# A hybrid decoder layer: expert down weights loaded by row blocks, and another order of the last gate chunk

## The chip, the cores and the metric

The kernel runs on one core of one Trainium2 chip. Its metric is the device time of one execution in microseconds (us). Five engines work on their own queues, each in the order of its instructions: TensorE (PE, with its weight loads as PEld), VectorE (DVE), ScalarE (ACT), GpSimd (POOL) and SyncE (SP), which issues nearly all loads. Data goes by 16 DMA engines between the chip's main memory and the on-chip memory.

## The reference

One decoder layer in float32 for 256 tokens of 2048 channels. What matters for the change is its second half:

```python
h = h + mixed @ w_out                       # conv and attention groups
xt = rms_norm(h, norm_ffn)
# each token: best of 4 groups, then the best 2 of the 8 experts in it
y_e = (silu(xt @ w_gate[e]) * (xt @ w_up[e])) @ w_down[e]      # e of 32, 2048 -> 512 -> 2048
h = h + sum over a token's two experts of weight * y_e
gate = sigmoid(rms_norm(h, norm_ple) @ w_ple_gate)             # 2048 x 2048
out = h + gate * (p @ w_ple)
```

All weights are read once: 479 MB in all, of which the experts have 403 MB.

## The kernel before

**Waves.** The 32 experts go in eight waves of four (`NW`). Each expert gets up to 32 tokens, gathered by a matmul with a selection matrix. The four experts of a wave share TensorE's array, each with its own group of 32 columns, so a product over four experts is four short matmuls side by side. A wave first makes gate and up (`gate_up`, L971), then the down product: hidden values of 512 channels, in four row blocks `j` of 128, against `w_down[e]`. For waves 0 to 3 the whole down product follows at once. For waves 4 to 7 only its first 1024 output columns do (`down_rows`, L1031); the other two chunks of 512 columns are made after wave 7 (`down_wave`, L1115), wave by wave, first chunk 2 (columns 1024 to 1535), then chunk 3. Each wave's result goes through `outputs` (a high part `yh` by ScalarE, a low part `yl` by VectorE, L1071 and L1072) and `scatter` (L1078), which returns it to token order in PSUM. `add_down` (L1123) adds a chunk's sum to the residual `acc`.

**The gate product.** It is made in chunks of 512 input rows: as soon as a chunk of the residual is final, `rows` transposes it (L1151) and splits it into a high and a low part `hs` (L1154, L1157, L1158); `squares` adds up its squares. A chunk has eight gate steps, numbered 0 to 23 over chunks 0 to 2 here and 24 to 31 in the last chunk: four column blocks `n` of 512, times two halves `q`. A step (`gate_step`, L1176 to L1178) is 12 matmuls of 512 columns, on a piece of `w_ple_gate` that `split` has divided into a high part (ScalarE copy, L347) and a low part (VectorE subtraction, L348). I call these split 0 to 31, by their steps. `prep_pg` issues the splits up to a given one, into three slots `wsl` used in turn; a split waits until the step that used its slot is done. After a column block of chunks 0 to 2 its sums are added to `gs` (L1202).

**Order at the end.** `steps(n)` issues the next `n` gate steps between other work. The gate steps of chunks 0 to 2 lie between the down products of waves 4 to 7. In the last chunk, `preload` (L1281) puts the `gs` collected so far into PSUM by a float32 matmul with the identity, two tiles per column block; the gate steps add to it. Then, per column block and token half: sigmoid (ScalarE, L1306), multiply by the `p` product (L1307), add to the residual (L1308), and a DMA to the output. The sigmoid's scale `rs5` needs the squares of all chunks: a reduction (L1291), a square root, a reciprocal, with a table load before the sigmoid.

**Slots and loads.** The on-chip memory has a ring of 26 slots of 1 MiB (`NSLOT`). `want` lists the loads in order, each 1 MiB; `free` gives slots back in program order and at once issues the next loads of the list on SP (L76). So a load is issued behind the release that its place in the program gives it. The list for waves 4 to 7: for each wave, gate and up, then eight half loads of `w_down` (first 1024 columns; one expert, two row blocks each, pieces of 4 KB); after wave 7, four column loads per wave and chunk (one expert, four row blocks each, pieces of 2 KB), with pairs of `w_ple_gate` loads between them by the list `halves_`.

**Nothing is reordered by a planner**: the kernel is written under a manual schedule, and each engine's instructions in the trace stand in the order in which the code issues them.

Of the kernel before, what the change touches and what calls it, by code (L numbers as in the profile page):

```python
# [8 lines left out]
F32R = mybir.dt.float32r  # L9
# [14 lines left out]
NSLOT = 26  # L24
# [6 lines left out]
def kernel(ctx: ExitStack, tc: tile.TileContext, I, out):  # L31
# [104 lines left out]
                         wt[e].rearrange("(p j) f -> p j f", j=16)[:, 4 * j4:4 * j4 + 4, :])  # L136

    def want_d(w, c0, n):
        for e in range(4 * w, 4 * w + 4):
            want(("d", e, c0), [128, 4, n], w_down[e].rearrange("(j p) n -> p j n", p=128)[:, :, c0:c0 + n])  # L140

    def want_rows(w):
        for j in range(4):
# [1 line left out]
                want(("r", e, j), [128, D], w_down[e, 128 * j:128 * j + 128, :])  # L145

    def want_halves(w):
        for jp in range(2):
            for e in range(4 * w, 4 * w + 4):
                want(("r", e, jp), [128, 2, 1024],  # L150
                     w_down[e, 256 * jp:256 * jp + 256, 0:1024].rearrange("(j p) n -> p j n", p=128))

    TC = [(0, 512), (512, 512), (1024, 512), (1536, 512)]
    w_pg_v = w_pg.rearrange("(k p) n -> p k n", p=128)
# [17 lines left out]
                want(("ple", k), [128, 2048], w_ple[128 * k:128 * k + 128, :])  # L172

    order = [(2, w) for w in range(NROW, NW)] + [(3, w) for w in range(NROW, NW)]
    halves_ = [(0, 1), (1, 0), (1, 1), (2, 0), None, (2, 1), None, (3, 0)]
    for (ci, w), nxt_ in zip(order, halves_):
        want_d(w, *TC[ci])
        if nxt_:
# [840 lines left out]
    def down_rows(w):  # L1019

        hv = hTw(w).rearrange("p (j s) -> p j s", j=4)
        nn = 4 if w < NROW else 2
        pts = [ps() for _ in range(nn)]

        def block(j, n):
            for e in range(4):
                if w < NROW:
                    d = arrived["r", 4 * w + e, j]
                else:
                    d = arrived["r", 4 * w + e, j // 2][:, j % 2]  # L1030
                nc.tensor.matmul(pts[n][32 * e:32 * e + 32, :], hv[:, j, 32 * e:32 * e + 32],  # L1031
                                 d[:, 512 * n:512 * n + 512], start=j == 0, stop=j == 3, tile_position=(0, 32 * e))

        def sums(n, y):
            ns = slice(512 * n, 512 * n + 512)
            po = pa()
            scatter(po, w, y, True, True)
            for tt in range(2):
                if w == 0:
                    if n == 0:  # L1040
                        macc[tt] = alloc([128, D], F32, "macc")
                    nc.vector.tensor_copy(macc[tt][:, ns], po[:, tt])
                else:
                    to = (hmid if w == NW - 1 else macc)[tt][:, ns]
                    nc.vector.tensor_add(to, po[:, tt], to)

        if w == NW - 1:
            for j in range(4):
                block(j, 0)
            y = outputs(pts[0], w)  # L1050
            for j in range(4):
                if j == 2:
                    sums(0, y)
                block(j, 1)
            free(8)
            y = outputs(pts[1], w)
            rows(0)
            sums(1, y)
            return
        for j in range(4):  # L1060
            for n in range(nn):
                block(j, n)
            if w < NROW or j % 2:
                free(4)
        for n in range(nn):
            sums(n, outputs(pts[n], w))

# [41 lines left out]
    def down_wave(w, c0, cn):  # L1109

        pt = ps()
        hv = hTw(w).rearrange("p (j s) -> p j s", j=4)
        for j in range(4):
            for e in range(4):
                nc.tensor.matmul(pt[32 * e:32 * e + 32, :], hv[:, j, 32 * e:32 * e + 32],  # L1115
                                 arrived["d", 4 * w + e, c0][:, j, :],
                                 start=j == 0, stop=j == 3, tile_position=(0, 32 * e))
        free(4)
        return outputs(pt, w)

    def add_down(po, c0, cn):
# [137 lines left out]
    rows(2)  # L1259
    steps(1)  # L1260
    squares(2)
    steps(3)
    po = pa()
    for w in range(NROW, NW):
        y = down_wave(w, *TC[3])
# [5 lines left out]
        scatter(po, w, y, w == NROW, w == NW - 1)  # L1271
        if w < NW - 1:
            steps(1)
    assert not todo
    early = [two(0), None, two(1), None]

    def preload(n):
        if early[n] is None:
            early[n] = two(n // 2)
        for tt in range(2):  # L1280
            nc.tensor.matmul(early[n][tt], ident, gs[tt][:, 512 * n:512 * n + 512], start=True, stop=False)  # L1281

    ci = last
    preload(0)
    add_down(po, *TC[ci])
    rows(ci)
    prep_pg(ci, 1)
    preload(1)
    preload(2)
    squares(ci)  # L1290
    nc.vector.tensor_reduce(rs5, ss5[:, :, 0:4], axis=AX.X, op=OP.add)  # L1291
    nc.scalar.activation(rs5, rs5, AF.Sqrt, bias=eps, scale=1.0 / D)
    nc.scalar.activation(junk, eps, AF.Sigmoid)
    nc.vector.reciprocal(rs5, rs5)
    so = [alloc([128, 4, 512], F32, "so") for _ in range(2)]
    for n in range(4):
        if n == 3:
            preload(3)
        for q in range(2):
            prep_pg(ci, 2 * n + q + 1)  # L1300
            gate_step(ci, 2 * n + q, early[n], False)
            prep_pg(ci, 2 * n + q + 2)
        ns = slice(512 * n, 512 * n + 512)
        for tt in range(2):
            sg = so[tt][:, n]
            nc.scalar.activation(sg, early[n][tt], AF.Sigmoid, scale=rs5[:, tt])  # L1306
            nc.vector.tensor_mul(sg, sg, ple[tt][:, ns])  # L1307
            nc.vector.tensor_add(sg, sg, acc[tt][:, ns])  # L1308
            nc.sync.dma_start(out[128 * tt:128 * tt + 128, ns], sg)
# [132 lines left out]
```

## Time and profile before

| | us |
|---|---|
| three runs | 1362.24, 1362.25, 1362.37 (median 1362.25) |
| the profiled execution | 1362.01 |
| its span, first to last instruction | 1360.3 |
| TensorE busy | 1137.8 (84%) |
| VectorE busy | 410.6 (30%) |
| ScalarE busy | 265.8 (20%) |
| DMA: 484.29 MB, mean 356 GB/s | |

Busy times overlap: they say how much an engine did, not what the end waited for. In the page's forty slices the DMA engines are full from about 380 us to 1320 us, and TensorE is nearly full again in the last 150 us. So the end of the kernel has to be read in the timeline of its last stage, engine by engine.

### The profile page before, as it was taken

The numbers are of one execution on the slowest core, as the hardware profiler recorded it, in microseconds if no ns is written. First come the engines' busy times: TensorE is split into PE (matmuls) and PEld (weight loads), VectorE is DVE, ScalarE is ACT, GpSimd is POOL, SyncE is SP. The second block draws the span as 40 slices with busy tenths as digits, with TensorE's granted clock in tenths as the row PEclk, the third lists the DMA queues.
The fourth block names the chain that finished last, engine by engine and source line by source line (L and its number), as shares of the span: only waits on it lengthen the run. The fifth ranks groups of instructions, "written<-read, shape, count | busy, mean of one in ns | idle before, by whom it ended". The sixth has DMA issues, their size and how long they took to land.

```text
span 1360.3 us, 14996 instructions
## 1 busy us (share of the span) xinstructions
PE 1137.8 (84%) x6171; PEld 633.3 (47%) x6172; DVE 410.6 (30%) x623; ACT 265.8 (20%) x435; POOL 122.6 (9%) x150
## 2 busy tenths in 40 slices
PE   8999899999998787668677775966986876689997
PEld 7888778888663251215125121511531511136655
DVE  6747877655411210201111020110110120124536
ACT  6435455544101000000000000000010000024324
POOL 2214577100000000000000000000000000000000
PEclk9999999999998888889879879998988988889999
DMA  8992245976899999999999999999999999999981
GB/s 261 311 343 80 77 154 175 376 240 221 345 421 420 421 421 421 421 422 420 422 421 421 422 421 422 414 420 421 414 420 421 415 420 422 414 396 394 392 339 63
DMA packets 133141, 484.29 MB, mean 356 GB/s; under 512 B 12020, under 2 KB 49292, under 8 KB 92876
## 3 DMA queue, kind: packets, MB, share of 16 engines
q1 hardware_dynamic: 131916, 480.37, 89.6%
q0 software_dynamic: 864, 2.40, 0.5%
q8 instruction: 50, 0.82, 0.2%
q10 hardware_dynamic: 288, 0.52, 0.2%
q14 instruction: 23, 0.19, 0.0%
HBM read 478.80 MB, written 4.19 MB: 355 GB/s over the span
## 4 chain that ended last, share of the span: by engine, by line
DMA 48%; PE 40%; DVE 5%; ACT 3%; issue 2%; SPq 1%; POOL 1%; ACTq 0%; DVEq 0%; POOLq 0%
DMA ld<-in_w_up_dram 33%; DMA ld<-in_w_down_dram 14%; PE pat L774 7%; PE pst L955 5%; PE pat L971 4%; PE pat L775 3%; PE pat L752 2%; PE pat L754 2%; PE pat L753 2%; PE pst L1115 2%; SPq L76 1%; PE pst L1098 1%; PE pst L1031 1%; DVE wsp L348 1%; PE pat L1078 1%
## 5 line engine op out<-in xcount | busy, mean ns | idle before, releaser
L971 PE MATMUL pat<-ld,xg 128*32 128x512 f32 x2048 | 328.2, 674 | 105.7 <-DMA ld<-in_w_up_dram 60.7
L971 PEld LDWEIGHTS pat<-ld,xg 128*32 128x32 f32 x2048 | 77.1, 121 | 345.9 <-issue 154.6
L774 PE MATMUL pat<-xs,wsp 128*128 128x512 f32 x544 | 197.1, 404 | 0.0
L1031 PE MATMUL pst<-ld,wv 128*32 128x512 f32 x768 | 151.9, 777 | 47.5 <-DMA ld<-in_w_down_dram 42.7
L775 PE MATMUL pat<-xs,wsp 128*128 128x256 f32 x544 | 154.0, 283 | 1.5 <-DVE wsp L348 1.5
L348 DVE TENSOR_TENSOR wsp<-ld,wsp 128x1024 fp32r<-128x1024 f32 x91 | 131.0, 1444 | 74.8 <-ACT wsp L347 74.8
L957 DVE TENSOR_TENSOR xg<-pst,gffn 128x512 f32<-128x512 f32 (+1 forms) x33 | 22.3, 676 | 400.1 <-PE pst L955 400.1
L347 ACT CAST wsp<-ld 128x1024 fp32r<-128x1024 f32 x104 | 107.9, 1048 | 87.2 <-PE pat L754 43.9
L955 PEld LDWEIGHTS pst<-sel,x 128*128 128x128 f32 x512 | 112.7, 311 | 8.4 <-issue 5.0
L774 PEld LDWEIGHTS pat<-xs,wsp 128*128 128x128 f32 x544 | 103.5, 190 | 27.8 <-issue 2.9
L955 PE MATMUL pst<-sel,x 128*128 128x128 f32 x512 | 114.8, 384 | 0.0
L1031 PEld LDWEIGHTS pst<-ld,wv 128*32 128x32 f32 x768 | 33.0, 135 | 160.4 <-DMA ld<-in_w_down_dram 80.8
L1008 ACT ACTIVATE sg<-pat 128x512 f32<-128x512 f32 x8 | 4.8, 597 | 523.3 <-PE pat L971 523.3
L775 PEld LDWEIGHTS pat<-xs,wsp 128*128 128x128 f32 x544 | 104.3, 192 | 2.4 <-DVE wsp L348 2.4
L1072 DVE SCALAR_TENSOR_TENSOR yl<-pst,sw,yh 128x512 fp32r<-128x512 f32 x32 | 23.9, 747 | 229.4 <-ACT yh L1071 229.4
L1071 ACT ACTIVATE yh<-pst,sw 128x512 fp32r<-128x512 f32 x32 | 22.0, 688 | 239.1 <-PE pst L1031 181.1
L948 POOL TENSOR_TENSOR sel<-sel,et 128x128 f32<-128x128 f32 x16 | 6.1, 400 | 643.2 <-DVE sel L946 643.2
L1078 PE MATMUL pat<-yl,wv 128*128 128x512 f32 x64 | 31.6, 493 | 27.4 <-DVE yl L1072 27.3
L752 PE MATMUL pat<-wsp,mx 128*128 128x512 f32 (+1 forms) x128 | 49.8, 389 | 0.1
L753 PE MATMUL pat<-wsp,mx 128*128 128x512 f32 (+1 forms) x128 | 49.0, 383 | 0.0
L754 PE MATMUL pat<-wsp,mx 128*128 128x512 f32 (+1 forms) x128 | 49.0, 383 | 0.0
L348 DVE TENSOR_TENSOR wsq<-ld,wsq 128x1024 fp32r<-128x1024 f32 x32 | 38.6, 1222 | 15.9 <-ACT wsq L347 15.9
(273 smaller groups left out, 1065.1 us busy)
## 6 DMA issues: line engine op xcount, KB each, us to landing
ld<-in_w_gate_dram SPq DMA_DIRECT2D x128, 1024.0 KB, 19.8
ld<-in_w_up_dram SPq DMA_DIRECT2D x128, 1024.0 KB, 11.1
ld<-in_w_down_dram SPq DMA_DIRECT2D x128, 1024.0 KB, 19.8
ld<-in_w_in_dram SPq DMA_DIRECT2D x35, 1024.0 KB, 13.1
ld<-in_w_out_dram SPq DMA_DIRECT2D x16, 1024.0 KB, 8.2
ld<-in_w_ple_gate_dram SPq DMA_DIRECT2D x16, 1024.0 KB, 17.1
spill<-x POOLq DMA_DIRECT2D x8, 256.0 KB, 4.8
ld<-in_w_ple_dram SPq DMA_DIRECT2D x2, 1024.0 KB
```

The source lines that it names most:

```text
L347: copy(t[:, :, 0], src)
L348: eng.tensor_sub(t[:, :, 1], src, t[:, :, 0].bitcast(F32))
L752: nc.tensor.matmul(o, mh, ws[:, kk, 0, cs], start=first, stop=False)
L753: nc.tensor.matmul(o, mh, ws[:, kk, 1, cs], start=False, stop=False)
L754: nc.tensor.matmul(o, ml, ws[:, kk, 0, cs], start=False, stop=last)
L774: nc.tensor.matmul(pt[:, b, :], ws[:, kk, 0, bs], xk, start=first, stop=False)
L775: nc.tensor.matmul(pt[:, b, 0:256], ws[:, kk, 1, bs], xk[:, 0:256], start=False, stop=last)
L955: nc.tensor.matmul(pt[:, 128 * jj:128 * jj + 128], hmid[tt][:, j::16], sel[w][:, tt], start=tt == 0, stop=tt == 1)
L971: nc.tensor.matmul(pt[32 * e:32 * e + 32, n, :], g[:, j, 32 * e:32 * e + 32], wt, start=j == 0, stop=j == 15, tile_position=(0, 32 * e))
L1031: nc.tensor.matmul(pts[n][32 * e:32 * e + 32, :], hv[:, j, 32 * e:32 * e + 32], d[:, 512 * n:512 * n + 512], start=j == 0, stop=j == 3, ti ...
L1078: nc.tensor.matmul(po[:, tt], sT(w)[:, 128 * tt:128 * tt + 128], y[i], start=start and i == 0, stop=stop and i == 1)
L1115: nc.tensor.matmul(pt[32 * e:32 * e + 32, :], hv[:, j, 32 * e:32 * e + 32], arrived["d", 4 * w + e, c0][:, j, :], start=j == 0, stop=j == ...
```

## The change

Four things change.

- **Loads of `w_down` in waves 4 to 7.** A column load holds one row block `j` of all four experts of the wave (was: one expert, four row blocks). A half load holds one row block of two experts (was: one expert, two row blocks). Bytes, number and piece length are the same. The products read them accordingly, and slots are freed after each row block: one for a column load, two for half loads.
- **Order of the list.** The second pair of `w_ple_gate` loads of chunk 2 comes after wave 6 of chunk 3 (was: after wave 5).
- **Gate steps.** Two of the three steps ahead of chunk 3's down products go; the steps of chunk 2 shift by two, and the last two stand after `add_down` and after `rows` of the last chunk.
- **The last chunk.** No preloads: gate steps start a new sum, and VectorE adds `gs` to it before the sigmoid, which now reads and writes on-chip memory. Up to five slots freed by then become extra split slots (`more`); splits up to number `more` are issued before the loop, the others inside it that many steps ahead.

```diff
--- before.py
+++ after.py
@@ -136,8 +136,9 @@
                          wt[e].rearrange("(p j) f -> p j f", j=16)[:, 4 * j4:4 * j4 + 4, :])
 
     def want_d(w, c0, n):
-        for e in range(4 * w, 4 * w + 4):
-            want(("d", e, c0), [128, 4, n], w_down[e].rearrange("(j p) n -> p j n", p=128)[:, :, c0:c0 + n])
+        for j in range(4):
+            want(("d", w, j, c0), [128, 4, n],
+                 w_down[4 * w:4 * w + 4, 128 * j:128 * j + 128, c0:c0 + n].rearrange("e p n -> p e n"))
 
     def want_rows(w):
         for j in range(4):
@@ -145,10 +146,10 @@
                 want(("r", e, j), [128, D], w_down[e, 128 * j:128 * j + 128, :])
 
     def want_halves(w):
-        for jp in range(2):
-            for e in range(4 * w, 4 * w + 4):
-                want(("r", e, jp), [128, 2, 1024],
-                     w_down[e, 256 * jp:256 * jp + 256, 0:1024].rearrange("(j p) n -> p j n", p=128))
+        for j in range(4):
+            for e in range(4 * w, 4 * w + 4, 2):
+                want(("r", e, j), [128, 2, 1024],
+                     w_down[e:e + 2, 128 * j:128 * j + 128, 0:1024].rearrange("e p n -> p e n"))
 
     TC = [(0, 512), (512, 512), (1024, 512), (1536, 512)]
     w_pg_v = w_pg.rearrange("(k p) n -> p k n", p=128)
@@ -172,7 +173,7 @@
                 want(("ple", k), [128, 2048], w_ple[128 * k:128 * k + 128, :])
 
     order = [(2, w) for w in range(NROW, NW)] + [(3, w) for w in range(NROW, NW)]
-    halves_ = [(0, 1), (1, 0), (1, 1), (2, 0), None, (2, 1), None, (3, 0)]
+    halves_ = [(0, 1), (1, 0), (1, 1), (2, 0), None, None, (2, 1), (3, 0)]
     for (ci, w), nxt_ in zip(order, halves_):
         want_d(w, *TC[ci])
         if nxt_:
@@ -1027,7 +1028,7 @@
                 if w < NROW:
                     d = arrived["r", 4 * w + e, j]
                 else:
-                    d = arrived["r", 4 * w + e, j // 2][:, j % 2]
+                    d = arrived["r", 4 * w + e // 2 * 2, j][:, e % 2]
                 nc.tensor.matmul(pts[n][32 * e:32 * e + 32, :], hv[:, j, 32 * e:32 * e + 32],
                                  d[:, 512 * n:512 * n + 512], start=j == 0, stop=j == 3, tile_position=(0, 32 * e))
 
@@ -1060,8 +1061,7 @@
         for j in range(4):
             for n in range(nn):
                 block(j, n)
-            if w < NROW or j % 2:
-                free(4)
+            free(4 if w < NROW else 2)
         for n in range(nn):
             sums(n, outputs(pts[n], w))
 
@@ -1113,9 +1113,9 @@
         for j in range(4):
             for e in range(4):
                 nc.tensor.matmul(pt[32 * e:32 * e + 32, :], hv[:, j, 32 * e:32 * e + 32],
-                                 arrived["d", 4 * w + e, c0][:, j, :],
+                                 arrived["d", w, j, c0][:, e, :],
                                  start=j == 0, stop=j == 3, tile_position=(0, 32 * e))
-        free(4)
+            free()
         return outputs(pt, w)
 
     def add_down(po, c0, cn):
@@ -1259,7 +1259,7 @@
     rows(2)
     steps(1)
     squares(2)
-    steps(3)
+    steps(1)
     po = pa()
     for w in range(NROW, NW):
         y = down_wave(w, *TC[3])
@@ -1271,39 +1271,35 @@
         scatter(po, w, y, w == NROW, w == NW - 1)
         if w < NW - 1:
             steps(1)
-    assert not todo
-    early = [two(0), None, two(1), None]
-
-    def preload(n):
-        if early[n] is None:
-            early[n] = two(n // 2)
-        for tt in range(2):
-            nc.tensor.matmul(early[n][tt], ident, gs[tt][:, 512 * n:512 * n + 512], start=True, stop=False)
+
+    assert nxt[0] == len(loads)
+    more = min(5, NSLOT - used[0])
+    wsl[:0] = [alloc([128, 2048], F32R, f"wsr{i}") for i in range(more)]
 
     ci = last
-    preload(0)
     add_down(po, *TC[ci])
+    steps(1)
     rows(ci)
     prep_pg(ci, 1)
-    preload(1)
-    preload(2)
+    steps(1)
+    assert not todo
     squares(ci)
     nc.vector.tensor_reduce(rs5, ss5[:, :, 0:4], axis=AX.X, op=OP.add)
     nc.scalar.activation(rs5, rs5, AF.Sqrt, bias=eps, scale=1.0 / D)
     nc.scalar.activation(junk, eps, AF.Sigmoid)
     nc.vector.reciprocal(rs5, rs5)
+    prep_pg(ci, more)
     so = [alloc([128, 4, 512], F32, "so") for _ in range(2)]
     for n in range(4):
-        if n == 3:
-            preload(3)
+        pt = two(n % 2)
         for q in range(2):
-            prep_pg(ci, 2 * n + q + 1)
-            gate_step(ci, 2 * n + q, early[n], False)
-            prep_pg(ci, 2 * n + q + 2)
+            gate_step(ci, 2 * n + q, pt, True)
+            prep_pg(ci, min(7, 2 * n + q + 1 + more))
         ns = slice(512 * n, 512 * n + 512)
         for tt in range(2):
             sg = so[tt][:, n]
-            nc.scalar.activation(sg, early[n][tt], AF.Sigmoid, scale=rs5[:, tt])
+            nc.vector.tensor_add(sg, pt[tt], gs[tt][:, ns])
+            nc.scalar.activation(sg, sg, AF.Sigmoid, scale=rs5[:, tt])
             nc.vector.tensor_mul(sg, sg, ple[tt][:, ns])
             nc.vector.tensor_add(sg, sg, acc[tt][:, ns])
             nc.sync.dma_start(out[128 * tt:128 * tt + 128, ns], sg)
```

## Rows read from the trace of the kernel before

**Rows 1.** Windows, three stages: us, busy us (instructions) per engine, clock, DMA share, GB/s

```profile
1250.00:1300.00 50.00, 49.49 (x267) 33.34 (x264) 27.56 (x33) 17.45 (x23) 0.00 (x0) 1.00 1.04 391
...
1300.00:1320.00 20.00, 20.00 (x116) 11.93 (x115) 6.03 (x8) 4.25 (x5) 0.00 (x0) 1.00 1.00 383
...
1340.00:1361.00 21.00, 12.98 (x54) 9.71 (x52) 11.05 (x15) 6.01 (x8) 0.00 (x0) 0.86 0.21 80
```

**Rows 2.** Timeline of TensorE's matmuls at the end: start us, us, instruction [idle before <-releaser]

```profile
1313.80 4.22 PE L1115 MATMUL pst<-ld,wv 128*32 128x512 f32 x32
...
1317.95 0.50 PE L1176 MATMUL pst<-wsq,hs 128*128 128x512 f32 x1
...
1321.75 1.88 PE L1281 MATMUL pat<-macc,ident 128*128 128x512 f32 x4
...
1324.31 1.31 PE L1151 MATMUL pst<-ident,x 128*128 128x128 f32 x8 [0.67 <-DVE x L1123]
...
1340.17 0.39 PE L1176 MATMUL pst<-wsq,hs 128*128 128x512 f32 x1
...
1345.62 1.88 PE L1281 MATMUL pst<-macc,ident 128*128 128x512 f32 x4
...
1352.59 0.39 PE L1178 MATMUL pst<-wsq,hs 128*128 128x512 f32 x1
```

**Rows 3.** Timeline of TensorE's weight loads, in wave 7's last down product

```profile
1314.39 0.14 PEld L1115 LDWEIGHTS pst<-ld,wv 128*32 128x32 f32 x5 [0.45 <-DMA ld<-in_w_down_dram]
```

**Rows 4.** Timeline of ScalarE at the end

```profile
1318.05 0.69 ACT L1071 ACTIVATE yh<-pst,sw 128x512 fp32r<-128x512 f32 x1 [9.15 <-PE pst L1115]
...
1320.16 1.03 ACT L347 CAST wsq<-ld 128x1024 fp32r<-128x1024 f32 x1
...
1325.73 0.62 ACT L1157 CAST hs<-tm 128x512 fp32r<-128x512 f32 x1 [4.53 <-DVE tm L1154]
```

**Rows 5.** Timeline of VectorE at the end

```profile
1321.23 1.23 DVE L348 TENSOR_TENSOR wsq<-ld,wsq 128x1024 fp32r<-128x1024 f32 x1 [1.70 <-ACT wsq L347]
...
1322.37 1.28 DVE L1202 TENSOR_TENSOR macc<-pst,macc 128x512 f32<-128x512 f32 x2
...
1323.57 1.28 DVE L1123 TENSOR_TENSOR x<-pat,x 128x512 f32<-128x512 f32 x2
...
1329.30 1.23 DVE L348 TENSOR_TENSOR wsq<-ld,wsq 128x1024 fp32r<-128x1024 f32 x1 [0.26 <-ACT wsq L347]
...
1330.54 0.16 DVE L1291 TENSOR_REDUCE rs<-ss 128x2 f32<-128x8 f32 x1
...
1333.52 2.36 DVE L348 TENSOR_TENSOR wsq<-ld,wsq 128x1024 fp32r<-128x1024 f32 x2 [2.29 <-ACT wsq L347]
...
1335.80 0.68 DVE L1307 TENSOR_TENSOR so<-so,ple 128x512 f32<-128x512 f32 x1
...
1336.52 0.69 DVE L1308 TENSOR_TENSOR so<-so,x 128x512 f32<-128x512 f32 x1
...
1337.13 0.68 DVE L1307 TENSOR_TENSOR so<-so,ple 128x512 f32<-128x512 f32 x1
...
1354.47 0.69 DVE L1308 TENSOR_TENSOR so<-so,x 128x512 f32<-128x512 f32 x1
```

**Rows 6.** Windows of 5 us: first experts' loads, a wait in wave 7, column loads

```profile
265.00:270.00 5.00, 5.00 (x24) 4.14 (x23) 3.77 (x4) 1.67 (x3) 0.00 (x0) 1.00 1.04 385
...
270.00:275.00 5.00, 5.00 (x24) 4.14 (x23) 2.45 (x2) 1.76 (x2) 0.00 (x0) 1.00 1.05 388
...
1185.00:1190.00 5.00, 3.53 (x5) 0.36 (x4) 1.97 (x2) 0.53 (x1) 0.00 (x0) 0.50 1.02 409
...
1270.00:1275.00 5.00, 5.00 (x27) 4.22 (x27) 2.98 (x5) 1.32 (x3) 0.00 (x0) 1.00 1.05 388
```

**Rows 7.** Timeline of SP's queue: the last loads of `w_out`

```profile
217.67 36.71 SPq L76 DMA_DIRECT2D ld<-in_w_out_dram  x14
```

**Rows 8.** Part 6 of the page: loads of `w_out`, last number us to landing

```profile
ld<-in_w_out_dram SPq DMA_DIRECT2D x16, 1024.0 KB, 8.2
```

## Prediction

> **What bounds the kernel now.** I read the stages first. [rows 1] The row of 1250 to 1300 us shows two things full at once: TensorE busy 49.5 of 50 us, and the DMA engines at a share of 1.04 with 391 GB/s. In 1300 to 1320 it is the same. In the last row (1340 to 1361) the DMA share is 0.21: the weights are in, and what is left is arithmetic. So there are two clocks: the stream of weights until about 1322 us, and a chain of engines behind it.
>
> Where the two meet I read in the timeline of the last down product of wave 7. TensorE starts it at 1313.80 [rows 2], loads weights for three experts, and stands 0.45 us until the fourth expert's tile is in, at 1314.39 [rows 3]. So TensorE runs right at the head of the stream there, and cannot pull that product ahead by having less to do: its data landed at 1314.4.
>
> Behind it the chain is: copy yh on ScalarE at 1318.05 [rows 4]; TensorE's gate step and scatter; `add_down` on VectorE at 1323.57 [rows 5]; transposes at 1324.31 [rows 2]; `hs`; split subtraction 25 at 1329.30; the reduction for `rs5` at 1330.54; a square root and the Sigmoid table on ScalarE, so that the next split subtraction starts at 1333.52; the first output operation at 1335.80; the last one from 1354.47 to 1355.16 [rows 5]. From that end to the end of the span (1360.3) are 5.1 us, from there to the profiled execution's 1362.01 another 1.7. I sum against 1362.01; it lies 0.24 us under the median of 1362.25. In these last 20 us TensorE paced the end: a pair of gate steps from 1340.17 to 1345.6 [rows 2], four subtractions and outputs of VectorE beside it.
>
> **The change, part by part.** One: the layout of the loads. Column loads (32 of them, waves 4 to 7, two chunks) and half loads (32) keep their count, bytes and piece length; only the four pieces of a partition now come from four experts (4 MiB apart) instead of four row blocks. No row shows these loads, but the first wave's gate and up loads step over four experts in the same way. They are the only ones issued after the last `w_out` load, at 254.4 us [rows 7]; with 8.2 us to landing [rows 8] the rows of 265 to 275 us are theirs: 385 and 388 GB/s, against 388 for column loads at 1270 to 1275 [rows 6]. A 1 MiB load takes 1.049 MB / 388 GB/s = 2.70 us either way. The upper bound is 32 x 2.70 x 3/388 = 0.7 us more; on the other side TensorE caps what a faster stream could give (rival three). I take nothing.
>
> The Trainium skill speaks against this part: the page "DMA: Bandwidth & Descriptors", section "Latency and other measured facts", says that a row pitch of 4 MiB per partition halves a DMA's rate (103 GB/s against 214). By that rule the column loads would cost about 86 us more; the first wave's rate above contradicts it where the step lies inside a partition, so the sum leaves it out.
>
> Two: slots freed after each row block. SP can issue earlier, but at a share of 1.04 an earlier issue only waits longer in the queue: 0, and if that cover were gone it could only gain. The pair of `w_pg` loads that swaps places with wave 6 of the last chunk stays ahead of wave 7's loads: these land when they did.
>
> Three: row blocks for wave 7. Before, the fourth expert's whole work (8 of 32 instructions, one column group, in series) came after the last landing: 1314.39 to 1317.95 = 3.56 us [rows 2, 3]. Now only row block 3 remains, 2 instructions per group: 3.56 x 2/8 = 0.9 us. Gain at `yh`: 2.65 us. TensorE is there in time: two gate steps (2.72 us each, half of 1340.17 to 1345.6) now come after it, so it reaches the product near 1308.
>
> Four: the order on VectorE behind it. Split 23 used to be made a wave earlier; now it stands between `yh` and the rest. ScalarE's `yh` falls to 1315.4, Sqrt table and split copy follow as before (2.11 us after `yh`, [rows 4]): copy 23 at 1317.5, its subtraction 1.07 later at 1318.6. Then in program order the sums of step 21, subtraction 24 and `add_down`: 1318.6 + 1.14 + 1.20 + 1.14 = 1322.06, with the start-to-start times of 1321.23, 1322.37 and 1323.57 [rows 5]. TensorE's step 21 and the scatter are done before (1315.3 + 3.80, which is 1317.95 to 1321.75 in [rows 2], = 1319.1). Against 1323.57 that is 1.51 us gained; 1.14 us of the 2.65 went to split 23. The first preload, 1.7 us, lay in TensorE's wait for `add_down`; its removal gives nothing here.
>
> Five: the rest up to `rs5`. Everything to subtraction 25 moves with it: 1329.30 - 1.51 = 1327.79. The step held back past the transposes adds its two sums on VectorE ahead of the reduction: 1327.79 + 1.14 + 1.20 = 1330.13, against 1330.54. TensorE is done with that step near 1326.7. Root and Sigmoid table follow (2.98 us): subtraction 26 at 1333.1, 0.4 us earlier than before.
>
> Six: the splits ahead. Thirteen slots are held for good and four by the last `w_pg` tiles, so 9 of 26 are free and `more` is 5. All six remaining splits (26 to 31) then stand in the queues before the first output; before, two did, the others between outputs. VectorE: 6 x 1.14 = 6.84 us, first output operation at 1339.95 instead of 1335.80. ScalarE's copies (1.03 us each at 1320.16, [rows 4]) keep ahead.
>
> Seven: outputs without preloads. Per output tile VectorE now has a sum from PSUM, waits for the sigmoid, multiplies and adds, and the next tile's sum is behind that add in its queue. Rows: sum 0.69 (as 1323.57, two in 1.28), hop 0.04, sigmoid from SBUF 0.62 (the 512-column ScalarE operation at 1325.73, [rows 4]; 0.69 from PSUM would be the other end), hop 0.03, multiply to add 0.72, add to the next operation 0.61 [rows 5]: 2.71 us. Eight of them, the last with its full end: 7 x 2.71 + 2.79 = 21.76 us, against 19.36 before (1335.80 to 1355.16), when ScalarE ran both sigmoids ahead. TensorE's pair of steps takes 5.45 us and VectorE's pair of tiles 5.42, so the late start is never made up. The other 5.2 us of preloads leave TensorE, which ends near 1350.9 (1352.98 - 0.41 - 1.72, [rows 2]) and waits for nobody; they are off the path.
>
> Sum: the last output operation ends at 1339.95 + 21.76 = 1361.7 instead of 1355.16, 6.55 us later (+4.15 start, +2.40 length). 1362.01 + 6.55 = **1368.6 us**.
>
> **The rivals.** One, not slower: VectorE does not wait for each sigmoid, since the other tile's sum covers it. Eight tiles then cost 8 x 1.98 = 15.9 us, the end is 1339.95 + 15.9, 0.7 us after 1355.16: 1362.7 us. For it: the two tiles are independent. Against it: VectorE's order in the trace is the order of the code throughout. It decides from where the first output starts before 1355.16 - 21.76 = 1333.4 us or the tiles overlap; subtraction 26 alone starts at 1333.1. Below it lies only TensorE's floor, with no wait for VectorE: 1355.16 - 0.41 (subtraction 26 earlier) - 1.72 (last preload) + 0.72 (sum) = 1353.75, or 1360.6 us.
>
> Two, slower still: TensorE at half clock behind wave 7. It will stand about 1.8 us before row blocks 2 and 3 (one load each 2.70, work 0.9). While it waited for tile after tile at 1185 to 1190 its granted clock was 0.50, the 1.2 GHz level [rows 6]. Row block 3 would take 0.9 and step 21 2.7 us longer, its sums start at 1321.9 instead of 1319.7: +2.2, 1370.8 us. Against it: it is busy without a gap until then.
>
> Three, less slow: the stream brings wave 7 earlier, and TensorE meets no wait. Then `yh` comes two steps and the 0.45 us wait earlier than 1318.05, at 1312.1 instead of 1315.4: -3.3, 1365.3 us. Against it: the same equal rates as above [rows 6].
>
> Four: loads over four experts take twice as long. 32 x 2.70 = 86 us on a full stream: 1455 us. Against it: the equal rates of [rows 6]. It is what the Trainium skill's rule on row pitch (page and section above) would give.
>
> **How the numbers follow.** Forecast 0.66 (own range 1366.5 to 1370); rival one 0.07, two 0.12, three 0.08, four 0.02; 0.05 for what I do not see. The range 1363 to 1373 holds rivals one in part, two and three, with the bounds of sigmoid (+0.6) and load rate (+0.7) on top. A change under 0.2% (2.7 us) cannot be told from none. Same: rival one and a part of three, 0.08; faster needs rival one and three together, 0.05; slower 0.87.
>
> **What would show it.** Down product of wave 7 done near 1315.3; `add_down` near 1322; six subtractions of 1.2 us in a row from 1333, ending about 1340; then VectorE busy to 1361.7 in the pattern sum, gap of 0.7, multiply, add; TensorE finished some 10 us before it. The prediction is wrong if VectorE's first output starts before 1335, if two sums stand side by side, if TensorE is the last to finish, or if the stream ends more than 3 us from 1322.

## The result, and the profile after

The changed kernel takes 1380.68 us (median of 4 runs, 1377.74 to 1381.51) against 1362.31 (4 runs, 1362.24 to 1363.34): a ratio of 1.0130, 95% interval 1.0116 to 1.0144. The direction was forecast, the size was not: 18.4 us were lost where 6.55 were expected, and the time lies above the range. The profiled execution took 1381.51 us, its span 1379.7.

The stages come first, in the same windows as [rows 1]. The columns are the stretch, its length, busy us (instructions) of PE, PEld, DVE, ACT and POOL, then the granted clock, the DMA share and GB/s:

```profile
1250.00:1300.00 50.00, 44.05 (x234) 27.60 (x235) 21.89 (x26) 13.76 (x19) 0.00 (x0) 0.93 1.02 362
1300.00:1320.00 20.00, 18.68 (x103) 11.07 (x102) 8.68 (x10) 4.95 (x6) 0.00 (x0) 1.00 1.03 389
...
1340.00:1361.00 21.00, 19.44 (x78) 15.39 (x77) 15.72 (x21) 10.55 (x17) 0.00 (x0) 0.92 0.07 26
```

Read the first row against the first of [rows 1]: the DMA share is as full as before (1.02 against 1.04), but the stream brings 362 GB/s instead of 391, and TensorE is idle for 6 of 50 us instead of 0.5. In these rows a full share says only that the DMA engines were occupied, not that they moved as much. The stretch of 1300 to 1320 is at its old rate; SP issues six loads of `w_ple_gate`, whose layout is unchanged, for it and into it, and how the rate divides between them and the column loads no row shows.

What this does to wave 7 stands in the weight loads of its last down product, where [rows 3] has one wait of 0.45 us, ended at 1314.39 (start, us, instruction, and in brackets idle time before and its releaser):

```profile
1316.58 0.16 PEld L1115 LDWEIGHTS pst<-ld,wv 128*32 128x32 f32 x8 [0.35 <-issue]
...
1318.40 0.16 PEld L1115 LDWEIGHTS pst<-ld,wv 128*32 128x32 f32 x8 [1.66 <-DMA ld<-in_w_down_dram]
...
1321.09 0.16 PEld L1115 LDWEIGHTS pst<-ld,wv 128*32 128x32 f32 x8 [2.53 <-DMA ld<-in_w_down_dram]
...
1325.20 0.20 PEld L1115 LDWEIGHTS pst<-ld,wv 128*32 128x32 f32 x8 [3.96 <-DMA ld<-in_w_down_dram]
```

Each row is one row block. The last one's tile is in at 1325.20, 10.81 us later than the last expert's tile before. Not all of it belongs to the column loads: wave 7's last half load was already 0.93 us late. The changed kernel's last two half loads, then the last one before:

```profile
1200.55 0.14 PEld L1032 LDWEIGHTS pst<-ld,wv 128*32 128x32 f32 x4 [2.37 <-DMA ld<-in_w_down_dram]
1203.13 0.20 PEld L1032 LDWEIGHTS pst<-ld,wv 128*32 128x32 f32 x8 [2.44 <-DMA ld<-in_w_down_dram]
```

```profile
1202.20 0.20 PEld L1031 LDWEIGHTS pst<-ld,wv 128*32 128x32 f32 x8 [2.42 <-DMA ld<-in_w_down_dram]
```

The stretch from there to the last tile, before and after (columns of the stages):

```profile
1202.20:1314.39 112.19, 111.05 (x608) 68.64 (x608) 53.31 (x63) 39.72 (x57) 0.00 (x0) 0.99 1.04 392
```

```profile
1203.13:1325.20 122.07, 109.44 (x596) 64.77 (x596) 51.03 (x60) 38.69 (x56) 0.00 (x0) 0.95 1.02 368
```

It takes 9.88 us more. By an estimate from these two rows, the 44.0 MB of before would take 7.3 us more at 368 GB/s; the other 2.6 us are 0.94 MB more that passed ahead of the last tile. The last wait shows such bytes: from 1321.09 to 1325.20 the stream ran at 394 GB/s (next fence), 1.6 MB for a tile of 1.05 MB. Which loads they belong to I did not follow up. TensorE had waited three times by then, and its clock was down (same columns as the stages):

```profile
1320.00:1325.00 5.00, 1.06 (x8) 0.16 (x8) 0.00 (x0) 0.00 (x0) 0.00 (x0) 0.74 1.03 394
...
1325.00:1330.00 5.00, 4.79 (x16) 2.59 (x17) 0.75 (x1) 2.76 (x4) 0.00 (x0) 0.57 0.75 303
```

The eight matmuls of each of the first three row blocks took 1.06 to 1.07 us (the clock of 1315 to 1320 is 1.00); those of the last took 1.94, at 0.57, near the 1.2 GHz level. So the product's copy starts 2.01 us after the landing. ScalarE, two rows:

```profile
1327.21 0.69 ACT L1071 ACTIVATE yh<-pst,sw 128x512 fp32r<-128x512 f32 x1 [12.11 <-PE pst L1115]
...
1352.45 0.72 ACT L1302 ACTIVATE so<-so,rs 128x512 f32<-128x512 f32 x1 [2.83 <-DVE so L1301]
```

And VectorE from there to its end (to be laid beside [rows 5]):

```profile
1330.38 1.23 DVE L349 TENSOR_TENSOR wsq<-ld,wsq 128x1024 fp32r<-128x1024 f32 x1 [1.70 <-ACT wsq L348]
1331.53 1.28 DVE L1202 TENSOR_TENSOR macc<-pat,macc 128x512 f32<-128x512 f32 x2
1332.72 1.22 DVE L349 TENSOR_TENSOR wsq<-ld,wsq 128x1024 fp32r<-128x1024 f32 x1
1333.86 1.28 DVE L1123 TENSOR_TENSOR x<-pat,x 128x512 f32<-128x512 f32 x2
...
1339.60 1.23 DVE L349 TENSOR_TENSOR wsr<-ld,wsr 128x1024 fp32r<-128x1024 f32 x1 [0.26 <-ACT wsr L348]
1340.74 1.28 DVE L1202 TENSOR_TENSOR macc<-pst,macc 128x512 f32<-128x512 f32 x2
1341.94 0.15 DVE L1287 TENSOR_REDUCE rs<-ss 128x2 f32<-128x8 f32 x1
...
1344.91 4.63 DVE L349 TENSOR_TENSOR wsr<-ld,wsr 128x1024 fp32r<-128x1024 f32 x4 [2.28 <-ACT wsr L348]
1349.45 2.35 DVE L349 TENSOR_TENSOR wsq<-ld,wsq 128x1024 fp32r<-128x1024 f32 x2
1351.72 0.69 DVE L1301 TENSOR_TENSOR so<-pat,macc 128x512 f32<-128x512 f32 x1
1353.20 0.69 DVE L1303 TENSOR_TENSOR so<-so,ple 128x512 f32<-128x512 f32 x1 [0.79 <-ACT so L1302]
1353.93 0.69 DVE L1304 TENSOR_TENSOR so<-so,x 128x512 f32<-128x512 f32 x1
1354.54 0.68 DVE L1301 TENSOR_TENSOR so<-pat,macc 128x512 f32<-128x512 f32 x1
...
1373.59 0.69 DVE L1304 TENSOR_TENSOR so<-so,x 128x512 f32<-128x512 f32 x1
```

The order is the forecast one, row by row: split 23, the sums of step 21, split 24, `add_down`; then the sums of the held-back step between split 25 and the reduction; six subtractions in a row; and tiles of sum, gap, multiply, add. The six subtractions take 6.8 us, one tile 2.82 (1351.72 to 1354.54), eight tiles 22.56 (1351.72 to 1374.28). VectorE ends last.

### The profile page after: what moved, and what is told of

The parts are those of the page before. It is cut to its first block, busy times and chain, and to the rows that moved or that the text cites. A ratio compares the mean times of both kernels' runs of the same rounds, so it can differ in the third digit from the quotient of the medians.

```text
span 1379.7 us, 14978 instructions
## 1 busy us (share of the span) xinstructions
PE 1137.5 (82%) x6155; PEld 630.7 (46%) x6156; DVE 414.8 (30%) x631; ACT 266.0 (19%) x435; POOL 122.9 (9%) x150
## 4 chain that ended last, share of the span: by engine, by line
DMA 54%; PE 34%; DVE 6%; ACT 3%; issue 2%; POOL 1%; SPq 0%; ACTq 0%; DVEq 0%; POOLq 0%
DMA ld<-in_w_up_dram 36%; DMA ld<-in_w_down_dram 16%; PE pat L775 6%; PE pst L956 5%; PE pat L972 4%; PE pat L776 3%; PE pat L753 2%; PE pat L754 2%; PE pat L755 2%; PE pst L1115 1%; DMA ld<-in_w_ple_dram 1%; DVE wsp L349 1%; PE pst L1032 1%; ACT wsp L348 1%; ACT S L500 1%
## 5 line engine op out<-in xcount | busy, mean ns | idle before, releaser
L972 PE MATMUL pat<-ld,xg 128*32 128x512 f32 x2048 | 342.4, 692 | 104.4 <-DMA ld<-in_w_up_dram 52.0
L1032 PE MATMUL pst<-ld,wv 128*32 128x512 f32 x768 | 138.8, 725 | 47.1 <-DMA ld<-in_w_down_dram 42.3
L1115 PE MATMUL pst<-ld,wv 128*32 128x512 f32 x256 | 32.1, 626 | 12.0 <-DMA ld<-in_w_down_dram 12.0
## 6 DMA issues: line engine op xcount, KB each, us to landing
ld<-in_w_up_dram SPq DMA_DIRECT2D x128, 1024.0 KB, 10.8
ld<-in_w_ple_gate_dram SPq DMA_DIRECT2D x16, 1024.0 KB, 18.4
```

The lines of the kernel that those rows point to most:

```text
L972: nc.tensor.matmul(pt[32 * e:32 * e + 32, n, :], g[:, j, 32 * e:32 * e + 32], wt, start=j == 0, stop=j == 15, tile_position=(0, 32 * e))
```

## The experiments

The two halves of the change can be taken apart: the layout of the loads, and the order at the end. The question was where the 12.9 us above the forecast come from, and then what about the layout costs the stream. One expert's `w_down` is 512 rows of 8 KB, 4 MiB in all; a row block of 128 rows is a stretch of 1 MiB of it. A column load reads a 2 KB piece of each of 512 rows. The minus lines of an edit are those of the run that it is compared with, and `...` marks a cut.

### The change with the old column loads

```diff
-        for j in range(4):
-            want(("d", w, j, c0), [128, 4, n],
-                 w_down[4 * w:4 * w + 4, 128 * j:128 * j + 128, c0:c0 + n].rearrange("e p n -> p e n"))
+        for e in range(4 * w, 4 * w + 4):
+            want(("d", e, c0), [128, 4, n], w_down[e].rearrange("(j p) n -> p j n", p=128)[:, :, c0:c0 + n])
```

The product and the release of slots follow it; half loads and all the rest stay as changed.

> The changed kernel with the column loads of before (one expert, four row blocks, four slots freed after the product); all else as changed. Theory A: in the changed kernel each of the 32 column loads took 3.04 instead of 2.70 us because its four pieces per partition step over four experts, 10.9 us in all; and, apart from that, the tail is late on VectorE. With the old loads the stream is back at 388 to 396 GB/s, wave 7's last tile lands near 1314.4 and yh starts near 1318.0 (the 2.65 us of row blocks are lost): sum over the predicted steps 1368.6 + 2.65 + 0.8 (tiles of 2.81 instead of 2.71 us) = 1372 us. Theory B, the tail alone made the kernel slower by 18 us and the stream waited for it: as slow as the changed kernel, 1378 to 1381.

Measured: 1374.90 us, ratio 1.0096 (1.0079 to 1.0113). The stream is back at its old rate, and the last tile lands at 1315.08; but TensorE then runs at half clock. Windows of this kernel, columns as before:

```profile
1250.00:1300.00 50.00, 48.92 (x266) 31.79 (x269) 24.93 (x30) 15.04 (x20) 0.00 (x0) 1.00 1.04 390
...
1315.00:1320.00 5.00, 4.92 (x26) 1.14 (x26) 0.00 (x0) 0.00 (x0) 0.00 (x0) 0.66 0.92 370
```

Its matmuls behind the last landing:

```profile
1315.08 5.30 PE L1114 MATMUL pst<-ld,wv 128*32 128x512 f32 x26 [1.67 <-DMA ld<-in_w_down_dram]
```

26 instructions take 5.30 us; at the 1.07 us for eight of the undisturbed row blocks they would take 3.5. The time lies 2.9 us above the first theory's sum; these 1.8 us and a landing 0.69 later than in [rows 3] are most of it. So the layout is the larger part of the surprise, and the rest of the change, above all the order at the end, costs 11.7 us (1374.90 against 1363.22), of which 1.8 are the clock.

### The kernel before with the new column loads

The same edit the other way round: `want_d`, the product's tile and `free()` per row block as in the change, nothing else.

> The kernel before with the new column loads alone (one row block of four experts, one slot freed after each block). Theory A: landing of wave 7's last tile near 1325 instead of 1314.4, yh near 1326.5 instead of 1318.05, the tail as before: 1370 to 1371 us, column loads at 340 to 360 GB/s. Theory B (not the loads): 1361.8 us, the half us of wait in wave 7 gone.

Measured: 1370.47 us, ratio 1.0052 (1.0034 to 1.0070), which the layout theory had named. Stream and last landing of this kernel:

```profile
1250.00:1300.00 50.00, 45.32 (x240) 30.29 (x236) 24.28 (x29) 15.15 (x20) 0.00 (x0) 0.97 1.01 354
...
1325.00:1330.00 5.00, 3.81 (x20) 2.52 (x21) 0.75 (x1) 2.65 (x4) 0.00 (x0) 1.00 0.83 338
```

```profile
1326.18 0.16 PEld L1116 LDWEIGHTS pst<-ld,wv 128*32 128x32 f32 x8 [3.28 <-DMA ld<-in_w_down_dram]
```

The landing is 11.8 us later than in [rows 3], and 2.65 by the forecast's working come back with the row blocks. That makes 9.15; the profiled executions differ by 9.16 (1371.17 against 1362.01), the medians by 7.25, since the runs of this kernel spread from 1367.37 to 1371.75. The two halves add up to the whole: 7.25 (this run) and 11.68 (the one above) make 18.93; the whole change measured 18.37.

### Four DMAs for a load, one expert each

If the 4 MiB steps inside one load were the cost, a load made of four DMAs, each on one expert's row block, should be free of it.

```diff
-                 w_down[4 * w:4 * w + 4, 128 * j:128 * j + 128, c0:c0 + n].rearrange("e p n -> p e n"))
+                 [w_down[e, 128 * j:128 * j + 128, c0:c0 + n] for e in range(4 * w, 4 * w + 4)])
```

> As e2, but each 1 MiB column load is issued as four DMAs of 256 KB, one expert each, into the same tile: same tiles, same releases, same bytes, only the order of the pieces differs. If the step from expert to expert between neighbouring pieces is what costs (theory A), the stream runs at 388 GB/s or a little under and the time is 1361.5 to 1363 us. If the finer releases or the order of issue cost (theory C), it is as slow as e2, 1370 to 1371 us.

Measured: 1393.39 us, ratio 1.0231 (1.0214 to 1.0248), outside both expectations:

```profile
1250.00:1300.00 50.00, 45.85 (x187) 26.68 (x190) 21.02 (x25) 12.79 (x17) 0.00 (x0) 0.93 0.96 310
```

The step inside a load is not needed for the loss: without it the rate falls further, to 310 GB/s. My reading fell, and two were left: that 256 KB DMAs are slow as such, or that it matters over how much of an expert's 4 MiB a DMA's rows are spread.

### Rows dealt out to the partitions

Here the hidden channels of waves 4 to 7 are dealt out so that partition p holds rows 4p to 4p+3 of an expert. A load still has four experts, 4 MiB apart, and 2 KB pieces, but its 128 rows are 32 KB apart and reach over all of an expert's 4 MiB.

```diff
-                 w_down[4 * w:4 * w + 4, 128 * j:128 * j + 128, c0:c0 + n].rearrange("e p n -> p e n"))
+                 w_down[4 * w:4 * w + 4].rearrange("e (p j) n -> p j e n", j=4)[:, j, :, c0:c0 + n])
...
-            nc.tensor.transpose(p2[:, 128 * j:128 * j + 128], hh[:, 128 * j:128 * j + 128], ident)
+            nc.tensor.transpose(p2[:, 128 * j:128 * j + 128],
+                                hh[:, 128 * j:128 * j + 128] if w < NROW else hh[:, j::4], ident)
```

This is on the kernel before with row blocks as above; its half loads are dealt out too.

> As e2 (one DMA, four experts per tile), but in waves 4 to 7 the 512 hidden channels are dealt out so that partition p holds rows 4p to 4p+3: the pitch from partition to partition is 32 KB, as in the first wave's expert loads that ran at 385 to 388 GB/s, instead of 8 KB; the step from expert to expert stays 4 MiB. Half loads are dealt out in the same way. If the pitch decides together with the step (theory A1), 1361.5 to 1363 us; if the 4 MiB step alone decides (A2), as e2, 1370 to 1371 us.

Measured: 1359.97 us (10 runs), ratio 0.9980 (0.9970 to 0.9989):

```profile
1250.00:1300.00 50.00, 50.00 (x279) 33.61 (x272) 27.82 (x34) 17.56 (x23) 0.00 (x0) 1.00 1.04 391
```

Full rate, with the same 4 MiB steps, the same number of DMAs and the same releases as the slow layout. The row blocks now give their gain: the time is 0.2% below the kernel before, under the range expected for it. Last landing and `yh`:

```profile
1316.29 0.16 PEld L1117 LDWEIGHTS pst<-ld,wv 128*32 128x32 f32 x8 [1.14 <-DMA ld<-in_w_down_dram]
```

```profile
1317.42 0.69 ACT L1073 ACTIVATE yh<-pst,sw 128x512 fp32r<-128x512 f32 x1 [9.01 <-PE pst L1117]
```

`yh` starts 1.13 us after the landing, where [rows 3] and [rows 4] have 3.66 (1314.39 to 1318.05).

### The two readings apart: skewed row blocks, and dealt rows in four DMAs

In the first, rows stay 8 KB apart, but at step j expert e gives row block `j ^ e`, so that a load touches all four quarters, one in each expert (two of the four steps need two DMAs of 512 KB):

```diff
-        for j in range(4):
-            want(("d", w, j, c0), [128, 4, n],
-                 w_down[4 * w:4 * w + 4, 128 * j:128 * j + 128, c0:c0 + n].rearrange("e p n -> p e n"))
+        for j in range(4):
+            a, b = 1 - 2 * (j // 2), 1 - 2 * (j % 2)
+            src = w_down[4 * w, 128 * j:128 * j + 128, c0:c0 + n]
+            rows_ = lambda i, m: bass.AP(tensor=src.tensor, offset=src.offset + i * (2 * DE + a * 256) * D,
+                                         ap=[list(src.ap[0]), [(DE + b * 128) * D, m], [1, n]])
...
-                nc.tensor.matmul(pt[32 * e:32 * e + 32, :], hv[:, j, 32 * e:32 * e + 32],
+                nc.tensor.matmul(pt[32 * e:32 * e + 32, :], hv[:, j ^ e, 32 * e:32 * e + 32],
...
```

> As e2 (the kernel before with column loads of four experts, pitch 8 KB between partitions), but at step j expert e gives row block j xor e, so that the four pieces of a partition lie 3 or 5 MiB apart and in four different row blocks (steps 1 and 2 as two DMAs of 512 KB). Theory S, from e2, e3 and e5: what costs is that all rows of a load lie in stretches of 1 MiB at the same place of each 4 MiB expert; then the skew heals it: 388 to 395 GB/s and 1360 to 1363 us. Theory A (the large step from expert to expert together with the 8 KB pitch): as e2, near 1370 us.

In the second, the dealt-out load is cut into four DMAs of 256 KB:

```diff
-                 w_down[4 * w:4 * w + 4].rearrange("e (p j) n -> p j e n", j=4)[:, j, :, c0:c0 + n])
+                 [w_down[e].rearrange("(p j) n -> p j n", j=4)[:, j, c0:c0 + n] for e in range(4 * w, 4 * w + 4)])
```

> As e5 (dealt rows, pitch 32 KB), but each column load issued as four DMAs of 256 KB, one expert each, as e3 did with rows of pitch 8 KB. Theory S: each DMA now spans the 4 MiB of its expert, so the stream stays near 390 GB/s, 1360 to 1363 us. If it was the number and size of the DMAs that made e3 slow (theory D), near 1390 us as e3.

Measured: 1361.65 us, ratio 0.9989 (0.9979 to 0.9999), and 1360.44 us, ratio 0.9987 (0.9977 to 0.9996). Skewed:

```profile
1250.00:1300.00 50.00, 50.00 (x275) 34.00 (x268) 28.61 (x35) 18.15 (x23) 0.00 (x0) 1.00 1.04 391
```

Dealt, four DMAs:

```profile
1250.00:1300.00 50.00, 50.00 (x277) 33.84 (x267) 28.26 (x34) 18.19 (x23) 0.00 (x0) 1.00 1.04 391
```

Both run at full rate. Neither the 8 KB distance of the rows (skewed has it) nor the size of the DMAs (the second has 256 KB) costs anything by itself. What the slow ones share is that all rows of a DMA lie in the same quarter of an expert: in the same 1 MiB of four experts 354 to 362 GB/s, in 1 MiB of one expert 310.

Two limits of this reading. The skew also changed the step from expert to expert, from 4 MiB to 3 or 5, and the four slow DMAs of a load followed one another at 4 MiB. So rows 8 KB apart together with a distance of 4 MiB, in one load or from one DMA to the next, are not excluded as the cause. And the quarter alone is not enough: the changed kernel's half loads, pieces of 4 KB, also lie in the same 1 MiB of two experts, and the last one landed 2.58 us after the one ahead of it (1200.55 to 1203.13), which is 406 GB/s. What in the memory makes the loss was not tried and stays open.

### The whole change with dealt-out rows

Everything of the change, but with loads that stream at the old rate: this is the kernel that the forecast's sum describes.

> The changed kernel whole, with the hidden channels of waves 4 to 7 dealt out as in e5 (pitch 32 KB), so that only the rate of its down loads differs. If the stream was the one step of the prediction that failed, wave 7's last tile lands near 1314.4 to 1315 and the rest follows as predicted, plus 0.1 us for each of eight output tiles and 1 to 2 us for TensorE's half clock at row block 3: 1369 to 1371 us. If the other steps fail too: 1375 us or more, or under 1366.

Measured: 1371.89 us (4 runs), ratio 1.0065 (1.0049 to 1.0082); the forecast for it was 1368.6. Stream and clock:

```profile
1250.00:1300.00 50.00, 48.61 (x275) 31.02 (x273) 24.91 (x30) 14.58 (x20) 0.00 (x0) 1.00 1.04 390
...
1315.00:1320.00 5.00, 3.90 (x13) 1.86 (x14) 0.75 (x1) 1.88 (x2) 0.00 (x0) 0.54 1.01 404
```

```profile
1316.10 1.93 PE L1116 MATMUL pst<-ld,wv 128*32 128x512 f32 x8 [1.64 <-DMA ld<-in_w_down_dram]
```

```profile
1323.00 1.29 DVE L1203 TENSOR_TENSOR macc<-pat,macc 128x512 f32<-128x512 f32 x2 [0.50 <-PE pat L1179]
...
1325.34 1.28 DVE L1124 TENSOR_TENSOR x<-pat,x 128x512 f32<-128x512 f32 x2
...
1343.57 0.69 DVE L1302 TENSOR_TENSOR so<-pat,macc 128x512 f32<-128x512 f32 x1
...
1365.45 0.69 DVE L1305 TENSOR_TENSOR so<-so,x 128x512 f32<-128x512 f32 x1
```

The time lies 0.9 us above the range expected for this run and 3.3 above the forecast, so the stream was the largest miss but not the only one. The last tile lands 1.71 us later than in [rows 3]; 1.68 of them stood already at wave 7's last half load (1203.88 against 1202.20), ahead of the column loads, and were not traced further. The last row block takes 1.93 us at a granted clock of 0.54, and step 21 behind it is late by 0.50 us for VectorE, as rival two has it. The first output starts at 1343.57, 3.62 after the forecast, and eight tiles take 22.57 us again.

### What the experiments point to

Dealt-out rows, two steps held back, the six splits (four of them now ahead of the square root), and outputs in pairs so that both sigmoids of a pair run behind both sums. The other steps fill TensorE's waits inside wave 7's product, so that it waits less; for column blocks 0 to 2 the last add goes to GpSimd.

```diff
+            if mid and j == 1:
+                mid()
...
+            nc.vector.tensor_add(so[tt][:, n], pt[tt], gs[tt][:, ns])
+        for tt in range(2):
+            nc.scalar.activation(so[tt][:, n], so[tt][:, n], AF.Sigmoid, scale=rs5[:, tt])
...
-            nc.vector.tensor_add(sg, sg, acc[tt][:, ns])
+            (nc.vector if n == 3 else nc.gpsimd).tensor_add(sg, sg, acc[tt][:, ns])
```

> f3 with another tail, to see whether VectorE's turn-taking with ScalarE is what made the changed kernel's end late: per column block both sums first, then both sigmoids, then multiplies, with the last add on GpSimd (1.3 us a tile) for blocks 0 to 2; splits 26 to 29 ahead of the square root and Sigmoid table; half loads as in e5; step 21 between row blocks 1 and 2 of wave 7's last product, step 22 ahead of the scatter, step 23 after the transposes. Sum: row block 3 done 1315.3, scatter 1319, add_down 1319.9, step 24 from 1323.9, eight steps of 2.73 to 1345.7, last output operation 3.5 us later at 1349.2 against 1355.16: 1356 us, TensorE last to finish. If VectorE still ends last: 1360 us or more.

Measured: 1359.64 us (10 runs), ratio 0.9979 (0.9969 to 0.9988): 0.2% below the kernel before, close to the second expectation (VectorE ends last), and not to be told apart from dealt-out rows alone (0.9980). Here the last tile's product runs at full clock; its landing and `yh`:

```profile
1314.68 0.16 PEld L1117 LDWEIGHTS pst<-ld,wv 128*32 128x32 f32 x8 [1.29 <-DMA ld<-in_w_down_dram]
```

```profile
1315.82 0.69 ACT L1073 ACTIVATE yh<-pst,sw 128x512 fp32r<-128x512 f32 x1 [6.58 <-PE pst L1117]
```

VectorE at its end:

```profile
1338.02 1.28 DVE L1304 TENSOR_TENSOR so<-pat,macc 128x512 f32<-128x512 f32 x2
1339.50 1.31 DVE L1309 TENSOR_TENSOR so<-so,ple 128x512 f32<-128x512 f32 x2 [0.20 <-ACT so L1306]
1340.72 1.28 DVE L1304 TENSOR_TENSOR so<-pst,macc 128x512 f32<-128x512 f32 x2
1342.20 2.16 DVE L1309 TENSOR_TENSOR so<-so,ple 128x512 f32<-128x512 f32 x2 [0.20 <-ACT so L1306]
...
1352.18 0.69 DVE L1310 TENSOR_TENSOR so<-so,x 128x512 f32<-128x512 f32 x1
```

GpSimd beside it:

```profile
1340.27 2.94 POOL L1310 TENSOR_TENSOR so<-so,x 128x512 f32<-128x512 f32 x2 [336.91 <-DVE so L1309]
```

TensorE's last matmul starts at 1346.35, but VectorE ends at 1352.87. The pair of multiplies without GpSimd beside most of it takes 1.31 us, the one that begins under GpSimd's adds 2.16, so some 0.85 us are given back there and in the next pair. The Trainium skill's page "SBUF — State Buffer", section "SBUF: two separate sides", says that a VectorE operation with two inputs in the on-chip memory is shut out while a GpSimd operation that reads there holds their shared port; the pair at 1342.20 agrees, and the sums at 1340.72, with one input from PSUM, keep their 1.28 us beside GpSimd, as the rule would have it.

## Why the prediction was wrong

**The step that failed is One.** It put the cost of the loads over four experts at nothing (0.7 us at most), because the first wave's loads step over four experts too and run at 385 to 388 GB/s [rows 6]. That row was the wrong neighbour. The first wave's rows are 32 KB apart in neighbouring partitions and reach over all of an expert's matrix, like the dealt-out rows, which are free; the column loads' 128 rows of an expert lie in one 1 MiB. I had compared only the step inside a partition, and with the rows dealt out this step costs nothing. What I left out is over which part of each matrix a load's rows lie: with all of them in the same 1 MiB of each expert the rate fell, with dealt-out or skewed rows it did not. The upper end was wrong with it, since it was worked out from the same rows. Measured: 10.81 us at the last landing. Of these 0.93 stood ahead of the column loads; the other 9.88 are 0.31 us for each of 32 column loads, by the estimate above 7.3 us from the lower rate and 2.6 from bytes that passed ahead of the last tile. Since the kernel's end waits for the last landing, all of it went into the time.

The sum against the profiled execution, from the forecast of 1368.6 to 1381.51, by the rows above:

| term | us |
|---|---|
| last landing, 1325.20 instead of 1314.39 (step One) | +10.81 |
| last row block at half clock: 2.01 us to `yh`, where the last kernel above, at full clock, has 1.14 (1314.68 to 1315.82) | +0.87 |
| the same at full clock: 1.14 instead of 1.01 (step Three) | +0.13 |
| `yh` to the first output: 24.51 instead of 24.55 (Four to Six) | -0.04 |
| eight tiles: 22.56 instead of 21.76 (Seven) | +0.80 |
| from the last output's end to the end: 7.23 instead of 6.85 | +0.38 |
| sum (1381.51 - 1368.56, the forecast before it was rounded) | +12.95 |

**Two** stands: earlier issues gave nothing that a row shows. **Three** was right in its mechanism: with dealt-out rows the kernel before has `yh` 1.13 us after the landing instead of 3.66, and the three runs of it at full rate gain 0.1 to 0.2%. **Four to Six** came out within 0.05 us over 24.5 us: `add_down` 6.65 us after `yh` (forecast 6.66), subtraction 26 at 11.05 after `add_down` (11.04), six subtractions in 6.81 (6.84). These were built from start-to-start times of the same operations, and held though everything was shifted by 11.8 us. **Seven** was right in pattern: no two sums stand side by side, VectorE ends last, TensorE some 10 us before. The tile is 2.82 instead of 2.71 us, since the sigmoid from the on-chip memory takes 0.72, the operation of [rows 4] that I took for it 0.62; even the end that I had named, 0.69, was too low. The direction does not rest on the stream: with dealt-out rows the change is still 0.65% slower, 0.48% by the forecast's numbers.

**The rivals.** Rival one did not happen. Rival three did not: three of the four tiles of the last product were waited for. Rival two did happen, at +0.87 in the changed kernel and with a late step 21 on top in the kernel with dealt-out rows. There the clock fell behind waits of the kind that the forecast itself had (about 1.8 us forecast, 1.61 and 1.64 measured); it deserved more than a chance of 0.12. In the kernel before with new columns, which waits once, the clock in the row behind its wait of 3.28 us is 1.00, so one such wait does not decide it; what does was not settled. Rival four had the right kind and the wrong size: 10.8 us instead of 86. The Trainium skill's rule on row pitch (page "DMA: Bandwidth & Descriptors", section "Latency and other measured facts") is of that kind, in that a power-of-two layout lowers the rate of a DMA whose bytes and count are unchanged. Its condition, a pitch of 4 MiB from partition to partition, stands in no run here: the loads with a 4 MiB step inside a partition and rows dealt out run at 391 GB/s, and the largest loss seen here is 310 against 391, not a half.

The bound at which I had called the prediction wrong (a stream that ends more than 3 us from 1322) was the right alarm, and it was this step that tripped it.

## What to carry to other kernels

When a change re-cuts a load and the stream bounds the kernel, compare its addresses with the nearest row's in every dimension, across the partitions as well as inside one, before its rate is borrowed; bytes, count and piece length alone do not fix the rate. Where a load by row blocks is wanted, deal the rows out so that each DMA covers the whole matrix: that costs one strided transpose and kept the rate. And a chain priced from start-to-start times of the same operations held when its start moved by 12 us (24.51 us for 24.55); where TensorE came late to it, with dealt-out rows, it took 25.47.

## What the runs showed of the hardware

- Loads of 2 KB pieces with equal bytes ran at different rates by where a DMA's rows lay: over all 4 MiB of a matrix 390 to 391 GB/s (rows 32 KB apart, or 8 KB apart in all four quarters), 8 KB apart with a different quarter for each expert 391, within the same 1 MiB of four matrices 354 to 362, within 1 MiB of one matrix 310. These are means over 50 us that hold some loads of `w_ple_gate` too. With 4 KB pieces, rows within the same 1 MiB of two matrices came at 406. The DMA share was 0.96 to 1.04 in all of the 50 us rows, so it hardly shows the loss.
- Cutting a 1 MiB load into four DMAs of 256 KB changed nothing where the rows were dealt out (391 GB/s).
- A pair of float32 multiplies on VectorE from the on-chip memory took 2.16 us beside GpSimd's adds and 1.31 with little of them beside it; GpSimd's two adds took 2.94.
- In three of the kernels TensorE's matmuls waited twice in a row for tiles, 1.61 to 3.05 us each with 1.04 to 1.06 us of matmuls between, and the clock granted around the matmuls that followed was 0.54 to 0.66 over 5 us. In a fourth a single wait of 2.37 us (3.28 in its weight loads) was followed by 1.00.
